# Turning xs with VectorE and ScalarE instead of TensorE in a Mamba-2 and attention trunk

## The chip, the cores and the metric

The kernel runs on one core of a Trainium2 chip. A core has five engines that work side by side, each through its own queue of instructions in order: TensorE (PE, matrix products, with its weight loads shown as PEld), VectorE (DVE), ScalarE (ACT), GpSimd (POOL) and SyncE (SP, which issues most of the DMAs). Operands lie in SBUF, a memory of 128 partitions; TensorE writes to PSUM, a second such memory. The metric is the device time of one execution in microseconds (us); lower is better.

## The reference

A trunk of two layers on x of 256 positions by 2048 features, float32. The first is a Mamba-2 mixer, the second a sliding-window attention mixer with shared keys and values; each ends in x <- LayerNorm(alpha * x + mixer(x)). The change lies in the first. Cut to what matters, that is:

```
zxbcdt = x @ w_in                     # 4096 z, 4096 xs, 1024 B, 1024 C, 64 dt
xbc = silu(causal_conv4(xs | B | C))
dt  = softplus(dt_raw + dt_bias);  da = dt * -exp(a_log)
cb      = C . B                       # per group: positions x positions
y_diag  = (cb * decay) @ (xs * dt)    # 8 heads a group, 64 features a head
y = y_diag + (the part from the chunk before) + xs * d_skip
y = y * silu(z);  y = rmsnorm_per_group(y) * norm_w;  out = y @ w_out
```

There are 8 groups of 8 heads, and two chunks of 128 positions. The kernel adds the part of the chunk before to the same product, with a decay over all 256 positions.

## The kernel before, in words

**Layout.** Activations of the first layer stand with features in the partitions and the 256 positions along the free axis. A weight block of 128 output features by 2048 inputs is loaded from DRAM in two halves of 128x1024 (tile wr), and each half is split into a high part that ScalarE rounds (wh, line L164) and a low part that VectorE subtracts (wl, L167). There are four buffers of wh, four of wl, six of wr. `load_next` keeps the splits two units ahead of their use.

**Blocks.** `block` makes one block of 128 features: 48 matmuls of 256 columns in `narrow` (L252), three for each of the 16 pieces of the input (high by high, low by high, high by low). Each group g has ten blocks: B, C, four blocks of xs (two heads each) and four of z. The first group takes three of its z blocks first, then B, C, the four xs and the last z. After a block of B, C or xs, `conv_silu` reads the PSUM tile: ScalarE scales (L492), VectorE adds three taps (L494), ScalarE takes tanh (L497) and VectorE closes (L498). After a block of z come L582 (ScalarE) and L583 (VectorE).

**What a group does.** `cb` multiplies C and B and masks (L590 to L592). `sum_decay` and `exp_decay` (L549, L557, ScalarE) make the decay e of the eight heads, `by_cb` (L597, VectorE) multiplies it by cb. `tr` (L607) turns the group's xs: TensorE transposes eight pieces of 128x128 into PSUM, and VectorE multiplies each of the four results by dt and writes it to xd (L612). `ymm` makes the products with xd as the stationary operand (L631), VectorE adds the skip part (L636, L642). `gate`, on GpSimd, multiplies by z and squares (L647 to L653); ScalarE and VectorE split the result into yH and yL (L661, L662). `norm` makes the scale of the group. The output blocks of the group (L323 to L325, 24 matmuls of 512 columns each) run in between the blocks of the next one.

**Order.** Two dictionaries, `plan` and `between`, say after (or within) which block each function is called. In the first group `tr` is called in block 11 (counted over all groups) and `ymm` after block 13; in the others `tr` after the group's eighth block and `ymm` after its tenth. The tile framework then orders the instructions of each engine by its own estimate of when their operands are ready, except for those that are held in program order (`pinned`, `keep_in_program_order`). The order of each engine's queue is fixed when the program is built.

**Buffers.** The tag yz has one buffer and holds the group's y; xd had four buffers of 256 columns. xs uses the tag sm, with seven.

Of the kernel before, what the change touches and what calls it, by code (L numbers as in the profile page):

```python
# [8 lines left out]
F32 = mybir.dt.float32  # L9
# [5 lines left out]
ALU = mybir.AluOpType  # L15
AX = mybir.AxisListType

P = 128
S = 256
# [36 lines left out]

BLOCKS = list(range(10))
BLOCKS0 = [6, 7, 8, 0, 1, 2, 3, 4, 5, 9]
CB_AT, TR_AT, Y_AT, NSM = 4, 7, 9, 7
B_ORDER = [("q", 0), ("g", 0), ("q", 1), ("g", 1), ("q", 2), ("o", 0), ("g", 2), ("q", 3),  # L60
           ("o", 1), ("g", 3), ("o", 2), ("o", 3)]

# [21 lines left out]
def trunk(ctx: ExitStack, tc: tile.TileContext, A: dict, out: bass.AP, dbg=None):  # L84
    nc = tc.nc
    PSUM = bass.MemoryType.PSUM

    def pool(name, bufs=1, side=None, space=None, stack=ctx):
        kw = {"space": space} if space is not None else {}
        return stack.enter_context(  # L90
            tc.tile_pool(name=name, bufs=bufs, side=side, reuse_waits="tile", **kw)
        )
# [9 lines left out]
    def nm(s):  # L102
        uid[0] += 1
        return f"{s}_{uid[0]}"

    def mm_tile():
        return mm_ps.tile([P, 512], F32, tag="mm", name=nm("mm"), bufs=4)

    def ax_tile():
        return ax_ps.tile([P, 512], F32, tag="ax", name=nm("ax"), bufs=4)  # L110

    cc = cst.tile([P, 1024], F32, tag="cc", name="cc")
    ident = cc[:, 0:128]
# [169 lines left out]
    ap = pool("ap", stack=w_stack)  # L283
# [25 lines left out]
    def pinned(m, pin):  # L309
        if pin:  # L310
            tc.keep_in_program_order(m)
# [86 lines left out]
    dtx = ap.tile([P, 2, NHD], F32, tag="dtx", name="dtx")  # L398
# [163 lines left out]
    gs = [G() for _ in range(NG)]  # L562
# [33 lines left out]
        e = es[g, hf]  # L596
        nc.vector.tensor_tensor(e[:], e[:], gs[g].cbm[:].unsqueeze(1).to_broadcast([P, 4, 384]), ALU.mult)  # L597

    def tr(g):
        st = gs[g]  # L600
        st.xd = {}
        for k in range(2):
            ps = ax_tile()
            for i in (2 * k, 2 * k + 1):
                for c in range(2):
                    o = (i % 2) * S + c * P
                    nc.tensor.transpose(ps[:, o : o + P], st.xs[i][:, c * P : (c + 1) * P], ident)  # L607
            for i in (2 * k, 2 * k + 1):
                o = (i % 2) * S
                xd = ap.tile([P, 2, 2, 64], F32, tag="xd", name=nm("xd"), bufs=4)  # L610
                hh = g * 8 + 2 * i
                m = nc.vector.tensor_tensor(  # L612
                    xd[:], ps[:, o : o + S].rearrange("p (c h d) -> p c h d", c=2, h=2),
                    dtx[:, :, hh : hh + 2].unsqueeze(3).to_broadcast([P, 2, 2, 64]), ALU.mult,
                )
                pinned(m, g == 0)
                st.xd[i] = xd

    def ymm(g):
        st = gs[g]  # L620
        st.yz = ap.tile([P, 4, S], F32, tag="yz", name=nm("yz"), bufs=1)
        for k in range(2):
            ps = ax_tile()
            for i in (2 * k, 2 * k + 1):
                o = (i % 2) * S
                xd = st.xd[i]
                for c in range(2):
                    cols = slice(o + c * P, o + S)
                    for r in range(2):
                        e = es[g, i // 2][:, 2 * (i % 2) + r, :]  # L630
                        nc.tensor.matmul(  # L631
                            ps[64 * r : 64 * r + 64, cols], xd[:, c, r, :], e[:, 256:] if c else e[:, :256],
                            start=c == 0, stop=c == 1,
                        )
            two = slice(2 * k, 2 * k + 2)
            nc.vector.tensor_tensor(  # L636
                st.yz[:, two, :], ps[:].rearrange("p (i q) -> p i q", i=2), els[g][:, two, :], ALU.mult
            )
            for i in (2 * k, 2 * k + 1):
                col = PC_D + g * 4 + i  # L640
                v = st.yz[:, i, :]
                nc.vector.scalar_tensor_tensor(v, st.xs[i][:], pc[:, col : col + 1], v, ALU.mult, ALU.add)  # L642
# [52 lines left out]
    def block(g, b):  # L695
# [15 lines left out]
        else:  # L711
            (in_b, in_c)[k](g, ps)

    visits = (turn_dt, cb, tr, ymm, norm)

    def group(g):
        for b in range(10):
# [75 lines left out]
    between = {}  # L793
# [6 lines left out]
    def at(t, fn, *a):  # L800
        plan.setdefault(t, []).append((fn, *a))
# [5 lines left out]
    for g in range(NG):  # L807
        t = 10 * g
        if g == 0:
            at(TD, turn_dt, *dts)  # L810
            at(4, load_decay, 0, 1)
            at(8, load_low, 0)
            pos = dict(cb=CB0, y=13)

            between[11] = [(tr, 0)]

            halves = [(5, 6, 7), (7, 8, 9)]
            by = (9, 10)
        elif g == 1:
            at(10, load_decay, 1, 0)  # L820
            at(10, load_decay, 1, 1)
            at(15, load_low, 1)
            pos = dict(cb=6, tr=TR_AT, y=Y_AT, norm=10 + CB_AT)

            halves = [(13, 14, 15), (15, 16, 16)]
            by = (16, 17)
        else:
            at(t - 5, load_decay, g, 0)
            at(t - 5, load_decay, g, 1)
            at(t, load_low, g)  # L830
            steps = t - 1
            pos = dict(cb=CB_AT, tr=TR_AT, y=Y_AT, norm=10 + CB_AT)
        for hf in range(2):
            if g < 2:
                sa, sb, ex = halves[hf]
                if (g, hf) != (1, 0):
                    at(sa, sum_decay, g, hf, 0, 2)
                at(sb, sum_decay, g, hf, 2, 4)
            else:
                at(steps + hf, sum_decay, g, hf)  # L840
                ex = steps + 1 + hf
            at(ex, exp_decay, g, hf)
        if g == 1:
            at(16, norm, 0)
        at(t + pos["cb"], cb, g)
        for hf in range(2):
            at(by[hf] if g < 2 else t + pos["cb"] + hf, by_cb, g, hf)
        if g > 0:
            at(t + pos["tr"], tr, g)
        at(t + pos["y"], ymm, g)  # L850
        if g == 0:
            at(t + pos["y"], sum_decay, 1, 0, 0, 2)
        for i in range(4):
            at(t + pos["y"], gate, g, i)
        if g > 0:
            at(t + pos["norm"], norm, g)
# [148 lines left out]
    for h in range(2):  # L1005
        ps = mm_tile()
# [277 lines left out]
    def cols(nb, c0=0, c1=512):  # L1284
        return slice(nb * 512 + c0, nb * 512 + c1)
# [67 lines left out]
    v = xr[:, 1, cols(3, 256)]  # L1353
# [102 lines left out]
```

## Time and profile before

| what | value |
|---|---|
| median of 3 runs | 987.62 us (987.59 to 988.2) |
| the profiled execution | 987.41 us, span 985.6 us |
| TensorE busy | 979.8 us (99%) |
| VectorE busy | 773.8 us (79%) |
| ScalarE busy | 611.9 us (62%) |
| GpSimd busy | 103.3 us (10%) |
| granted TensorE clock | 1.00 |
| transposes of L607 | 64, busy 8.3 us in all |
| scalings of L612 | 32, busy 11.9 us in all |

The profile is of one execution on the chip. A row of the groups of instructions names the line, the engine, the operation, what it writes and reads, the shape and the count; then its busy time in us and the mean duration of one in ns; then the engine's idle time just ahead of these instructions and what ended it. A row of the timeline has the start in us, the duration in us, and the instruction; "x10" means that ten in a row are merged. An instruction of an engine can begin before the last one has ended, so the distance between two starts can be shorter than a duration. The ends of matmuls are modelled; their starts are measured.

### The profile page before, as it was taken

How to read it: one execution, taken by the hardware profiler on the slowest of the kernel's cores; microseconds unless marked ns; L12 is line 12 of the kernel's file. 1: busy time of each engine (PE TensorE's matmuls, PEld its weight loads, DVE VectorE, ACT ScalarE, POOL GpSimd, SP SyncE). 2: the span in 40 equal slices, each digit the busy share in tenths (PEclk: the TensorE clock that was granted, in tenths of full speed). 3: DMA queues.
4: the chain of work that ended last, by engine and by line, in shares of the span. 5: the costliest groups of instructions: out<-in, count | busy, mean ns of one | idle time of the engine just before them, and what ended most of it. 6: DMA issues, size and time to landing. Idle time of an engine off the chain costs nothing.

```text
span 985.6 us, 18078 instructions
## 1 busy us (share of the span) xinstructions
PE 979.8 (99%) x7068; PEld 890.7 (90%) x7068; DVE 773.8 (79%) x1194; ACT 611.9 (62%) x1108; POOL 103.3 (10%) x137
## 2 busy tenths in 40 slices
PE   9999999999999999999999999999999999999998
PEld 8999989999999998999999999888898978978976
DVE  7898897877786787786787688789867678766786
ACT  7595866547655654663763665467467777764772
POOL 0001303004003001200300300303100000000003
PEclk9999999999999999999999999999999999999999
DMA  9788587565666656656657466458655646564642
GB/s 357 263 286 303 171 273 212 173 223 176 206 222 184 227 194 201 206 175 227 201 174 225 141 219 207 140 171 277 222 164 164 189 157 196 157 211 145 203 140 85
DMA packets 61556, 198.89 MB, mean 202 GB/s; under 512 B 6848, under 2 KB 11360, under 8 KB 61216
## 3 DMA queue, kind: packets, MB, share of 16 engines
q1 hardware_dynamic: 58528, 188.53, 58.4%
q0 software_dynamic: 2336, 8.69, 2.8%
q8 instruction: 55, 0.90, 0.4%
q10 hardware_dynamic: 608, 0.52, 0.2%
q14 instruction: 29, 0.24, 0.1%
HBM read 195.49 MB, written 2.23 MB: 201 GB/s over the span
## 4 chain that ended last, share of the span: by engine, by line
PE 99%; DVE 0%; DVEq 0%; issue 0%
PE mm L252 54%; PE mm L976 11%; PE mm L323 9%; PE mm L324 9%; PE mm L325 9%; PE ax L631 2%; PE ax L607 1%; PE ax L1116 1%; PE ax L1109 0%; PE ax L590 0%; PE mm L390 0%; PE ax L1233 0%; PE ax L1219 0%; PE ax L1066 0%; PE ax L907 0%; PE ax L372 0%
## 5 line engine op out<-in xcount | busy, mean ns | idle before, releaser
L167 DVE TENSOR_TENSOR wl<-wr,wh 128x1024 fp32r<-128x1024 f32 (+2 forms) x338 | 393.8, 1184 | 104.2 <-ACT wh L164 100.9
L164 ACT ACTIVATE wh<-wr 128x1024 fp32r<-128x1024 f32 (+2 forms) x338 | 333.1, 1011 | 146.6 <-PE mm L252 58.4
L252 PE MATMUL mm<-xH,wh 128*128 128x256 f32 x1280 | 355.4, 278 | 0.0
L252 PE MATMUL mm<-xL,wh 128*128 128x256 f32 x1280 | 354.1, 277 | 0.0
L252 PE MATMUL mm<-xH,wl 128*128 128x256 f32 x1280 | 353.9, 276 | 0.0
L252 PEld LDWEIGHTS mm<-xH,wh 128*128 128x128 f32 x1280 | 240.7, 188 | 1.8 <-issue 0.5
L252 PEld LDWEIGHTS mm<-xL,wh 128*128 128x128 f32 x1280 | 240.6, 188 | 1.0
L252 PEld LDWEIGHTS mm<-xH,wl 128*128 128x128 f32 x1280 | 240.5, 188 | 0.0
L323 PE MATMUL mm<-wh,yH 128*128 128x512 f32 x256 | 101.4, 396 | 0.0
L324 PE MATMUL mm<-wh,yL 128*128 128x512 f32 x256 | 99.8, 390 | 0.0
L325 PE MATMUL mm<-wl,yH 128*128 128x512 f32 x256 | 99.7, 389 | 0.0
L647 POOL TENSOR_TENSOR yz<-yz,z 128x256 f32<-128x256 f32 x32 | 32.7, 1032 | 470.7 <-DVE yz L642 470.7
L252 PE MATMUL mm<-x1H,wh 128*128 128x256 f32 x256 | 71.9, 281 | 0.0
L494 DVE SCALAR_TENSOR_TENSOR cv<-mm,pc,cv 128x255 f32<-128x255 f32 x144 | 68.8, 478 | 3.3 <-ACT cv L492 1.9
L252 PE MATMUL mm<-x1L,wh 128*128 128x256 f32 x256 | 71.1, 278 | 0.0
L252 PE MATMUL mm<-x1H,wl 128*128 128x256 f32 x256 | 71.0, 278 | 0.0
L976 PE MATMUL mm<-wh,x1H 128*128 128x512 f32 x160 | 63.1, 394 | 0.0
L976 PE MATMUL mm<-wl,x1H 128*128 128x512 f32 x160 | 61.8, 389 | 0.0
L976 PE MATMUL mm<-wh,x1L 128*128 128x512 f32 x160 | 60.9, 390 | 0.0
L323 PEld LDWEIGHTS mm<-wh,yH 128*128 128x128 f32 x256 | 48.1, 188 | 10.3 <-DVE z L583 1.0
L325 PEld LDWEIGHTS mm<-wl,yH 128*128 128x128 f32 x256 | 48.1, 188 | 10.2
L332 DVE SCALAR_TENSOR_TENSOR xr<-mm,r,xr 128x512 f32<-128x512 f32 x64 | 47.1, 746 | 11.7 <-PE mm L325 7.3
(228 smaller groups left out, 1375.8 us busy)
## 6 DMA issues: line engine op xcount, KB each, us to landing
wr<-in_wa SPq DMA_DIRECT2D x154, 512.0 KB, 5.0
wr<-in_wo SPq DMA_DIRECT2D x64, 512.0 KB, 4.4
wr<-in_wq SPq DMA_DIRECT2D x32, 512.0 KB, 4.4
wr<-in_wg SPq DMA_DIRECT2D x31, 512.0 KB, 5.0
wr<-in_wb SPq DMA_DIRECT2D x16, 512.0 KB, 4.5
wr<-in_wb SPq DMA_DIRECT2D x32, 256.0 KB, 3.8
rb<-rscr SPq DMA_DIRECT2D x11, 512.0 KB, 4.1
wr<-in_wkv SPq DMA_DIRECT2D x8, 512.0 KB, 5.1
```

The lines of the kernel that those rows point to most:

```text
L164: m = nc.scalar.activation(h[:, sl], v, AF.Copy)
L167: m = nc.vector.tensor_tensor(l[:, sl], v, h[:, sl].bitcast(F32), ALU.subtract)
L252: m = nc.tensor.matmul(ps, a, b, start=first and i == 0, stop=last and i == 2)
L323: pinned(nc.tensor.matmul(ps, aH[:, k, hs], u.h[:, ks], start=k == 0 and add is None, stop=False), pin)
L324: pinned(nc.tensor.matmul(ps, aL[:, k, hs], u.h[:, ks], start=False, stop=False), pin)
L325: pinned(nc.tensor.matmul(ps, aH[:, k, hs], u.l[:, ks], start=False, stop=k == 3), pin)
L332: nc.vector.scalar_tensor_tensor(v, ps, rms[:, h : h + 1], v, ALU.mult, ALU.add)
L494: nc.vector.scalar_tensor_tensor(a[:, sft:], ps[:, : S - sft], w(3 - sft), a[:, sft:], ALU.mult, ALU.add)
L607: nc.tensor.transpose(ps[:, o : o + P], st.xs[i][:, c * P : (c + 1) * P], ident)
L631: nc.tensor.matmul(ps[64 * r : 64 * r + 64, cols], xd[:, c, r, :], e[:, 256:] if c else e[:, :256], start=c == 0, stop=c == 1,)
L647: nc.gpsimd.tensor_tensor(v, v, st.z[i][:], ALU.mult)
L976: m = nc.tensor.matmul(ps[:], (x1H, x1L, x1H)[i][:, kk, hs], (u.h, u.h, u.l)[i][:, ks], start=(kk, i) == (0, 0), stop=ui == 3 and (k, i) = ...
```

## The change

xs is no longer turned by TensorE. `turn_xs` has VectorE transpose each of the four xs tiles of a group (128x256) in blocks of 32x32 into zx, a tile in yz's buffer. A block transpose leaves each block in the partitions where it was, so `carry_xs` copies the blocks to the partitions where they belong: 16 copies of 32 partitions by 256 elements on ScalarE, from quarter i of the partitions of zx to quarter j of those of xd. `scale_xs` then multiplies the whole of xd (128x1024) by dt in place, with one instruction of VectorE. xd is one tile with one buffer, and `ymm` reads it from there. The turn stands after block 9 in the first group and after the seventh block of each other group; the copies stand there and after the one or two blocks behind it; the scaling is two blocks behind the turn (three in the first group, where it is held in program order).

```
-    def tr(g):
-        ...
-                    nc.tensor.transpose(ps[:, o : o + P], st.xs[i][:, c * P : (c + 1) * P], ident)
-        ...
-                m = nc.vector.tensor_tensor(
-                    xd[:], ps[:, o : o + S].rearrange("p (c h d) -> p c h d", c=2, h=2),
-                    dtx[:, :, hh : hh + 2].unsqueeze(3).to_broadcast([P, 2, 2, 64]), ALU.mult,
-                )
+    def turn_xs(g):
+        st = gs[g]
+        st.zx = ap.tile([P, 4, 8, 32], F32, tag="yz", name=nm("zx"), bufs=1)
+        for i in range(4):
+            nc.vector.transpose(st.zx[:, i].rearrange("p f b -> p (f b)"), st.xs[i][:])
+        st.xd = ap.tile([P, 2, 4, P], F32, tag="xd", name=nm("xd"), bufs=1)
+    def carry_xs(g, js):
+        st = gs[g]
+        z = st.zx[:].rearrange("p i (c j) b -> p j c i b", c=2)
+        for j in js:
+            for i in range(4):
+                nc.scalar.copy(st.xd[32 * j : 32 * j + 32, :, :, 32 * i : 32 * i + 32], z[32 * i : 32 * i + 32, j])
+    def scale_xs(g):
+        v = gs[g].xd[:].rearrange("p c i (h d) -> p c (i h) d", h=2)
+        d = dtx[:, :, g * 8 : g * 8 + 8].unsqueeze(3).to_broadcast([P, 2, 8, 64])
+        pinned(nc.vector.tensor_tensor(v, v, d, ALU.mult), g == 0)
...
-                            ps[64 * r : 64 * r + 64, cols], xd[:, c, r, :], e[:, 256:] if c else e[:, :256],
+                            ps[64 * r : 64 * r + 64, cols], st.xd[:, c, i, 64 * r : 64 * r + 64], e[:, 256:] if c else e[:, :256],
...
-            between[11] = [(tr, 0)]
+            xs_at = 9
...
         if g > 0:
-            at(t + pos["tr"], tr, g)
+            xs_at = t + 6
+        at(xs_at, turn_xs, g)
+        for n, js in enumerate(((0,), (1,), (2, 3)) if g < 2 else ((0, 1), (2, 3))):
+            at(xs_at + n, carry_xs, g, js)
+        at(xs_at + 2 + (g == 0), scale_xs, g)
```

In the changed kernel the block transposes are line L604, the copies L613 and the scaling L618; the later lines of the file move by three.

More of the change, by code (lines that the diff above doesn't have):

```diff
@@ L58 @@
 BLOCKS0 = [6, 7, 8, 0, 1, 2, 3, 4, 5, 9]
-CB_AT, TR_AT, Y_AT, NSM = 4, 7, 9, 7
+CB_AT, Y_AT, NSM = 4, 9, 7
 B_ORDER = [("q", 0), ("g", 0), ("q", 1), ("g", 1), ("q", 2), ("o", 0), ("g", 2), ("q", 3),
@@ L597, in by_cb @@
         nc.vector.tensor_tensor(e[:], e[:], gs[g].cbm[:].unsqueeze(1).to_broadcast([P, 4, 384]), ALU.mult)
-    def tr(g):
+    def turn_xs(g):
         st = gs[g]
[L601 to L612, printed above, removed]
-                    xd[:], ps[:, o : o + S].rearrange("p (c h d) -> p c h d", c=2, h=2),
-                    dtx[:, :, hh : hh + 2].unsqueeze(3).to_broadcast([P, 2, 2, 64]), ALU.mult,
-                )
-                pinned(m, g == 0)
-                st.xd[i] = xd
+        st.zx = ap.tile([P, 4, 8, 32], F32, tag="yz", name=nm("zx"), bufs=1)
[12 more added lines that the diff above has]
+        pinned(nc.vector.tensor_tensor(v, v, d, ALU.mult), g == 0)
     def ymm(g):
@@ L625, in ymm @@
                 o = (i % 2) * S
-                xd = st.xd[i]
                 for c in range(2):
@@ L712, in block @@
             (in_b, in_c)[k](g, ps)
-    visits = (turn_dt, cb, tr, ymm, norm)
+    visits = (turn_dt, cb, ymm, norm)
     def group(g):
@@ L822, in trunk @@
             at(15, load_low, 1)
-            pos = dict(cb=6, tr=TR_AT, y=Y_AT, norm=10 + CB_AT)
+            pos = dict(cb=6, y=Y_AT, norm=10 + CB_AT)
             halves = [(13, 14, 15), (15, 16, 16)]
@@ L831, in trunk @@
             steps = t - 1
-            pos = dict(cb=CB_AT, tr=TR_AT, y=Y_AT, norm=10 + CB_AT)
+            pos = dict(cb=CB_AT, y=Y_AT, norm=10 + CB_AT)
         for hf in range(2):
```

## The prediction

> **What bounds the kernel now.** I read the page's busy shares first, then its chain of work.
>
> ```profile
> span 985.6 us, 18078 instructions
> PE 979.8 (99%) x7068; PEld 890.7 (90%) x7068; DVE 773.8 (79%) x1194; ACT 611.9 (62%) x1108; POOL 103.3 (10%) x137
> ...
> PE 99%; DVE 0%; DVEq 0%; issue 0%
> ```
>
> TensorE is the bound, and the chain that ended last runs on it from end to end. So a matmul taken away is worth its full pitch, and a microsecond in which TensorE waits costs a microsecond. The other engines count only where they make it wait. The busy time of each engine by stretch shows where that is near (columns: PE, PEld, DVE, ACT, POOL busy and instructions, clock, DMA share, GB/s):
>
> ```profile
> 58.00:76.00 18.00, 18.00 (x159) 17.95 (x158) 16.85 (x22) 16.12 (x28) 1.06 (x2) 1.00 0.84 284
> 76.00:94.00 18.00, 18.00 (x167) 17.13 (x166) 15.24 (x27) 8.31 (x12) 0.00 (x0) 1.00 0.93 354
> 310.00:390.00 80.00, 80.00 (x620) 75.50 (x619) 60.56 (x80) 45.89 (x68) 8.49 (x10) 1.00 0.62 199
> ```
>
> In the first group (about 58 to 94 us) VectorE is 85 to 94% busy, and ScalarE 90% in the first half. A later group (310 to 390) leaves VectorE 19 us and ScalarE 34 us idle. The change will be decided in the first group.
>
> **What the change removes: eight transposes a group on TensorE.** The timeline of TensorE around those of one group:
>
> ```profile
> 287.14 0.28 PE L252 MATMUL mm<-xH,wl 128*128 128x256 f32 x1
> 287.25 1.04 PE L607 MATMUL ax<-cc,xs 128*128 128x128 f32 x8
> 288.05 0.36 PE L252 MATMUL mm<-xH,wh 128*128 128x256 f32 x1
> 288.25 0.28 PE L252 MATMUL mm<-xL,wh 128*128 128x256 f32 x1
> 288.37 0.28 PE L252 MATMUL mm<-xH,wl 128*128 128x256 f32 x1
> ```
>
> Eight transposes hold the array from 287.25 to 288.05, 0.80 us. The matmul after them takes 0.20 us to the next start where 0.113 is usual (288.25 to 288.37, and 48 of them make a block of 5.45 us): 0.08 more. So 0.88 us a group, 8 x 0.88 = 7.0 us. Nothing else on TensorE changes in number: the products of L631 keep their shapes.
>
> **What it adds on VectorE and ScalarE.** The groups of instructions by shape (busy us, mean ns | idle before):
>
> ```profile
> L612 DVE TENSOR_TENSOR xd<-ax,dtx 128x256 f32<-128x256 f32 x32 | 11.9, 419 | 6.9 <-PE ax L607 6.8
> L1158 DVE STREAM_TRANSPOSE z<-p 128x1024 f32<-128x1024 f32 x8 | 9.9, 1239 | 0.0
> L1150 DVE TENSOR_TENSOR p<-p,sm 128x1024 f32<-128x1024 f32 x8 | 9.8, 1226 | 0.3
> L1177 ACT COPY ptw<-z 32x256 f32<-32x256 f32 x56 | 22.6, 404 | 9.6 <-DVE z L1158 8.9
> L1129 ACT COPY p<-ax 128x256 f32<-128x256 f32 x16 | 4.7, 382 | 0.0
> L661 ACT ACTIVATE yH<-yz,pc 128x256 fp32r<-128x256 f32 x32 | 16.3, 510 | 33.2 <-POOL yz L647 33.2
> L647 POOL TENSOR_TENSOR yz<-yz,z 128x256 f32<-128x256 f32 x32 | 32.7, 1032 | 470.7 <-DVE yz L642 470.7
> ```
>
> VectorE loses four L612 a group (0.33 us apart, 1.32) and gains four block turns and one scaling. A turn of 1024 columns takes 1.24 us, as the elementwise L1150 does; so one of 256 is put at L612's 0.42, 0.33 apart. The scaling of 128x1024 from SBUF is L1150's 1.23. Sum: 1.3 + 1.15 - 1.3 = 1.2 us more a group. ScalarE gains 16 copies of 32x256. L1177 is the same kind, 32 partitions to 32 others, at 0.404. L1129, which writes in pieces of 32 columns as the new copies do, takes 0.382 over 128 partitions; so the pieces cost nothing. The dearest row for 256 columns from SBUF is L661's 0.51, my upper bound. How close together do they run?
>
> ```profile
> 735.60 2.00 ACT L164 ACTIVATE wh<-wr 128x1024 fp32r<-128x1024 f32 x2
> ...
> 739.89 4.12 ACT L1177 COPY pt<-z 32x256 f32<-32x256 f32 x10
> 744.03 2.10 ACT L164 ACTIVATE wh<-wr 128x128 fp32r<-128x128 f32 x3
> ```
>
> Two L164 (1.05 each by their group) end in 2.00: the second starts 0.1 before the first ends. Ten copies take 4.14 to the next start, 0.414 each: none starts before the last one ended. The Trainium skill, "VectorE: DVE Perf Modes", section "Two Vector instructions with no wait between them", says that an instruction whose operands start in another quarter of the partitions than the last one's is held until that has finished. It tells this of VectorE alone, and the row shows it on ScalarE; read as the page has it, the copies would run 0.31 apart and my sum would be 984.2 instead of 986.2. I take the row: 16 x 0.414 = 6.6 us a group, as every new copy changes its quarter.
>
> No DMA is added, removed or moved; SP's and GpSimd's queues are as before. The new buffer zx shares yz's slot, so VectorE's first turn of a group waits for GpSimd's gating of the group before. That is eleven instructions of at most L647's 1.03, so some 11 us after the products; the first turn follows the next group's third block, 16 us after them: hidden.
>
> **Groups 2 to 7.** The copies stand behind ScalarE's reading of the seventh block, the scaling behind them. In one group that reading and the products were these:
>
> ```profile
> 282.10 0.36 ACT L582 ACTIVATE z<-mm 128x256 f32<-128x256 f32 x1
> ```
>
> ```profile
> 304.60 2.82 PE L631 MATMUL ax<-e,xd 128*64 128x256 f32 x32
> ```
>
> Between them lie 22 us. The copies' 6.6, two weight splits of 0.95 among them and 1.2 of scaling need 10. ScalarE has 34 us idle a group to take 6.6 from, so the splits keep ahead too, and the gain of 0.88 is kept in each group.
>
> **Group 0, where it is lost.** The timelines of TensorE, ScalarE and VectorE before:
>
> ```profile
> 88.00 2.82 PE L631 MATMUL ax<-e,xd 128*64 128x256 f32 x32
> ```
>
> ```profile
> 68.11 0.42 ACT L497 ACTIVATE xs<-cv 128x256 f32<-128x256 f32 x1 [1.69 <-DVE cv L494]
> ...
> 72.42 1.99 ACT L164 ACTIVATE wh<-wr 128x1024 fp32r<-128x1024 f32 x2
> 74.31 0.55 ACT L492 ACTIVATE cv<-mm,pc 128x256 f32<-128x256 f32 x1
> 74.76 1.05 ACT L164 ACTIVATE wh<-wr 128x1024 fp32r<-128x1024 f32 x1
> 79.11 0.42 ACT L497 ACTIVATE bt<-cv 128x256 f32<-128x256 f32 x1 [3.29 <-DVE cv L494]
> ```
>
> ```profile
> 79.56 0.43 DVE L498 SCALAR_TENSOR_TENSOR bt<-bt,cv 128x256 f32<-128x256 f32 x1 [0.55 <-ACT bt L497]
> 79.91 1.41 DVE L612 TENSOR_TENSOR xd<-ax,dtx 128x256 f32<-128x256 f32 x4
> ...
> 90.46 0.42 DVE L498 SCALAR_TENSOR_TENSOR xs<-xs,cv 128x256 f32<-128x256 f32 x1 [0.54 <-ACT xs L497]
> ```
>
> TensorE reaches the first group's products at 88.00. In the changed order ten matmuls of the next block stand ahead of them, so it gets there at 88.00 - 0.88 + 10 x 0.113 = 88.2. What it needs is the scaled xd. Before, L612 had made that by 81.3, out of PSUM. In the changed order of VectorE the scaling stands behind L498 of the second group's first xs block, which ran at 90.46. If nothing ahead of it moved, the scaling would end at 90.46 + 0.34 + 1.23 = 92.0: 3.8 us too late. And it does move:
> - ScalarE: eight copies, one split's two halves and three copies now stand ahead of L492 (74.31), five more copies behind it. Eleven copies add 4.6; a split half (0.95) has gone behind L492; the idle 1.69 at 68.11 is gone, since VectorE now does the stencil of the fourth xs block earlier. L492 starts at 74.31 + 4.6 - 0.95 - 1.6 = 76.4.
> - Its three stencils on VectorE wait for each other (0.55 each), then the tanh waits behind five copies (2.1) and a split half: L498 of bt at about 81.2, 1.6 later than 79.56.
> - From there to L498 of xs were 10.9 us, nearly all busy. Four L612 leave (1.3) and a fifth split half comes in (1.1): again some 10.9, so 92.2.
> The scaling runs from 92.5 to 93.7 and TensorE starts the products at 93.8: **a gap of 5.6 us**.
>
> **Group 1** has the least to spare after that. A low half at 122.02 is done at 124.37, its first reader starts at 125.80:
>
> ```profile
> 122.02 2.35 DVE L167 TENSOR_TENSOR wl<-wr,wh 128x1024 fp32r<-128x1024 f32 x2
> ```
>
> ```profile
> 125.80 0.28 PE L252 MATMUL mm<-xH,wl 128*128 128x256 f32 x1
> ```
>
> 1.4 us spare. Four turns come in ahead and 13 copies in a row; TensorE comes 4.8 us later (the gap less 0.88). Walked in the same way, 0.4 us is left: no wait, but barely.
>
> **The sum**, on the profiled execution: 987.41 (span 985.6 and 1.8 around it) - 7.0 + 5.6 = 986.0. That execution stands 0.2 below the median of the runs, 987.62; so **986.2 us**, 0.14% faster. A measurement of this kernel can tell about 0.2%, so this is no change.
>
> **Bounds.** Each 0.1 us on a copy moves the gap by 1.6. Copies 0.31 apart give a gap of 3.6 and 984.2; copies of 0.51 one of 7.2 and 987.8. Turns as dear as 0.78 would cost 2 us, partly in group 1.
>
> **The rivals.**
> - The clock falls in the gap (0.30). TensorE starts the program at half pace:
>
> ```profile
> 1.00 2.95 PE L372 MATMUL ax<-zero 128*128 128x512 bf16 x7 [1.00 <-DVE zero L360]
> ...
> 5.35 0.41 PE L252 MATMUL mm<-xH,wh 128*128 128x256 f32 x1
> 5.56 0.37 PE L252 MATMUL mm<-xL,wh 128*128 128x256 f32 x1
> 5.77 0.28 PE L252 MATMUL mm<-xH,wl 128*128 128x256 f32 x1
> 5.89 0.28 PE L252 MATMUL mm<-xH,wh 128*128 128x256 f32 x1
> ```
>
> Starts are 0.21 apart until 5.77, then 0.12, after work from 1.0 on: 4.8 us at half pace, 2.4 us lost. TensorE idles 5.8 us in the whole span before (979.8 of 985.6), most of it at its ends, so no row tells how long an idle stretch has to be. The matmul stream goes on at full pace after the waits of tenths of a microsecond that the rows show, and starts at half pace after the long rest before the program; 5.6 us lies between, so the chance is not far below the forecast's. If it is enough, 986.2 + 2.4 = 988.6 (987.4 to 990). The Trainium skill, "TensorE: Matmul & The Clock Gate", section "Why this matters for your kernels", warns of idle gaps over some 3 us: one idle window puts the clock back to half. By that rule the forecast would be 988.6 in those runs in which a whole window falls into the gap; the start of the trace agrees, and no run here shows the fall.
> - A second gap in group 1 (0.18), the case on the slower side: VectorE over 0.4 us later than walked at the split of 122 us, because 13 copies in a row keep ScalarE's halves back. Each us beyond 0.4 costs one; from 1.8 us the kernel is slower than before, from 3.8 by over 0.2%. It speaks for it that the spare time was 1.4 even before; against it, that ScalarE and VectorE work on while TensorE stands in the first gap. 988 to 993.
> - The gap is smaller or absent (0.14): copies overlap (984.2), or the scaling comes in time (980.6). Against it is the order: L618 stands behind an instruction at 90.46.
>
> **How the numbers follow.** The forecast, with gap and full clock, has 0.38 and its own range 985.2 to 987.6. 980.6 and 993 are the outer ends; cut to eight in ten: 983 to 991. Faster than 985.6: most of the small-gap case and a quarter of the forecast, 0.25. Slower than 989.6: two thirds of the second gap and the upper part of the clock case with some room for what I don't see, 0.25. Within: 0.50.
>
> **What would show it.** No L607 on TensorE; L631 of group 0 starting near 93.8, with some 5.6 us idle ahead, released by VectorE's L618; L613 x16 in each group with starts 0.41 apart; each later group 0.88 us shorter. TensorE's starts behind the gap 0.21 apart would be the clock; an idle stretch near 129 the second gap; L618 before 90 or L613 far from 0.40 would make the walk wrong.

## The result, and the profile after

The changed kernel takes 989.82 us, median of 20 runs (987.17 to 991.69); the kernel before, on the same chip, 987.80 (987.35 to 989.18). The ratio is 1.0018, with a 95% interval of 1.0011 to 1.0025: slower by 2 us, where 986.2 had been forecast. The profiled execution took 990.41 us, 3.0 more than that of before.

The head of the page and its chain that ended last, changed kernel:

```profile
span 988.6 us, 18074 instructions
...
PE 975.7 (99%) x7004; PEld 885.2 (90%) x7004; DVE 781.8 (79%) x1202; ACT 662.7 (67%) x1236; POOL 103.8 (10%) x137
...
PE 93%; ACT 3%; DMA 2%; DVE 1%; issue 1%; DVEq 0%; ACTq 0%
```

TensorE has its 64 transposes less and is 4.1 us less busy, yet the span is 3.0 longer. The chain, which ran on TensorE from end to end before, now goes through ScalarE, a DMA and VectorE first: somewhere TensorE waited for them. The timeline of TensorE has the place:

```profile
88.61 0.28 PE L252 MATMUL mm<-xH,wh 128*128 128x256 f32 x1
96.02 5.39 PE L631 MATMUL ax<-e,xd 128*64 128x256 f32 x32 [7.12 <-DVE xd L618]
101.33 0.38 PE L252 MATMUL mm<-xL,wh 128*128 128x256 f32 x1
```

Two things stand in it. From the last matmul to group 0's products are 7.40 us, released by the scaling L618: a gap, where the forecast had one, but longer than its 5.6. And the 32 products take 5.39 us, where they took 2.82 before. The table of stretches says why (columns: length, PE busy and instructions, granted clock, DMA share, GB/s):

```profile
80.00:91.00 11.00, 8.89 (x79) 1.00 0.81 269
91.11:101.35 10.24, 5.33 (x33) 0.50 0.78 276
101.35:120.00 18.65, 18.65 (x154) 1.00 0.43 133
```

The clock fell to one half 2.5 us behind the start of the last matmul ahead of the gap and came back 5.3 us after work had begun again. The sum closes on the spans: 7.0 saved, 7.40 - 0.11 lost in the gap, 5.39 - 2.82 = 2.57 lost at half pace; -7.0 + 7.3 + 2.6 = +2.9, and the spans differ by 3.0. The mean granted clock was 0.994 to 0.997 in every one of the 20 runs, and 0.999 to 1.0 in 93 of the 95 runs of before that were taken beside the experiments (0.998 and 0.997 in the other two). The products keep the line L631 in the changed file.

### The profile page after: what moved, and what is told of

Same layout as the page of the kernel before. It is cut to its first block, busy times and chain, and to the rows that moved or that the text cites. A ratio compares the mean times of both kernels' runs of the same rounds, so it can differ in the third digit from the quotient of the medians.

```text
span 988.6 us, 18074 instructions
## 1 busy us (share of the span) xinstructions
PE 975.7 (99%) x7004; PEld 885.2 (90%) x7004; DVE 781.8 (79%) x1202; ACT 662.7 (67%) x1236; POOL 103.8 (10%) x137
## 4 chain that ended last, share of the span: by engine, by line
PE 93%; ACT 3%; DMA 2%; DVE 1%; issue 1%; DVEq 0%; ACTq 0%
PE mm L252 49%; PE mm L979 11%; PE mm L323 9%; PE mm L324 9%; PE mm L325 9%; PE ax L631 2%; ACT wh L164 1%; DMA rb<-rscr 1%; ACT xd L613 1%; PE ax L1119 1%; ACT e L549 1%; DMA wr<-in_wa 0%; PE ax L1112 0%; DVE wl L167 0%; PE mm L390 0%
## 5 line engine op out<-in xcount | busy, mean ns | idle before, releaser
L497 ACT ACTIVATE xs<-cv 128x256 f32<-128x256 f32 x32 | 13.3, 416 | 69.7 <-DVE cv L494 69.7
L325 PEld LDWEIGHTS mm<-wl,yH 128*128 128x128 f32 x256 | 48.1, 188 | 10.2
```

Source lines behind the costliest of these rows:

```text
L325: pinned(nc.tensor.matmul(ps, aH[:, k, hs], u.l[:, ks], start=False, stop=k == 3), pin)
L497: nc.scalar.activation(dst, a[:], AF.Tanh)
```

## The experiments

Two claims of the forecast were to be tried first, the 0.88 us a group and the loss in group 0; then what each part of the loss costs. The theory held after the result: the gap comes from the place of the scaling on VectorE, and the clock falls in it and costs as well. The main rival: the gap alone costs, and the half clock is covered by something else.

### Groups 1 to 7 alone, group 0 alone

```
+            if g == 0:
+                between[11] = [(tr, 0)]     # TensorE's turn, as before, into the single xd
+            else:
                 at(xs_at, turn_xs, g)
                 ...
```

The second kernel has it the other way round: group 0 the new way, the others by `tr`.

> The first group keeps its transposes on TensorE (written into the one xd tile); groups 1 to 7 are as in the changed kernel. Theory (the loss is the first group's late scaling and the clock that falls in the wait): seven gains of 0.88 us, no wait of several us, clock 1.00; 987.7 - 6.2 = 981.5, at most 982.5. Rival (the 16 copies a group cost ScalarE, and so TensorE, something in every group): the loss is spread over the groups, seven eighths of it stay, 989 to 990.

> Only the first group is turned in the new way; groups 1 to 7 keep their transposes. Theory: one gain of 0.88, a wait of 5.6 to 7.4 us ahead of the first group's products and 2 to 4 us for the fallen clock; 994 to 998. Rival (cost in every group): one eighth of the change's effect, 987.5 to 988.5.

Measured, beside 987.75 us for the kernel before on the same chip: groups 1 to 7 alone 982.74 us (982.68 to 984.62, 5 runs), ratio 0.9952 (0.9940 to 0.9965), at a clock of 0.999 to 1.0. Group 0 alone 995.92 (995.55 to 997.06, 4 runs), ratio 1.0083 (1.0069 to 1.0097). So the change gains 5 us in seven groups and loses 8 in the first. Group 0 alone shows the gap and the half pace again, in TensorE's timeline (L649 and L636 are the products and the scaling in this file):

```profile
95.74 5.22 PE L649 MATMUL ax<-e,xd 128*64 128x256 f32 x32 [6.98 <-DVE xd L636]
```

By the same sum: -0.9 for its eight transposes, 7.25 - 0.11 for the gap, 5.22 - 2.82 for the pace, together +8.6; the medians differ by 8.2.

Groups 1 to 7 gain 7 x 0.88 = 6.2 less a wait of 1.16 us that comes up in group 1 (122.32 to 123.48):

```profile
122.32 0.39 PE L325 MATMUL mm<-wl,yH 128*128 128x512 f32 x1
123.48 0.50 PE L323 MATMUL mm<-wh,yH 128*128 128x512 f32 x1 [0.77 <-DVE xr L332]
```

The usual distance between two such matmuls is 0.23 us, so the wait costs 0.9: 987.75 - 6.2 + 0.9 = 982.5, and 982.74 was measured. In the changed kernel the first gap hides this wait. So its +2.0 us is group 0's +8.2 less the whole 6.2 of the seven others.

### The scaling of group 0 set free, or planned one block earlier

```
-        pinned(nc.vector.tensor_tensor(v, v, d, ALU.mult), g == 0)
+        pinned(nc.vector.tensor_tensor(v, v, d, ALU.mult), False)
```

```
-        at(xs_at + 2 + (g == 0), scale_xs, g)
+        at(xs_at + 2, scale_xs, g)
```

> All eight groups new; the first group's scaling is not held in program order, so that it stands on VectorE ahead of L498 of block B of the second group. Theory: the wait ahead of the first group's products goes (xd ready by about 81 us, before TensorE comes at 87), the clock stays at 1.00; 980.6 if TensorE waits nowhere else, 984 if the later gating of the first group keeps its norm (a wait of up to 2.7 us near 109 us). Rival (cost in every group): the place of one scaling changes little, 988 to 990.

> All eight groups new; the first group's scaling is called one block earlier (after block 11) and still held in program order, so that it stands behind L498 of block C of the second group, five microseconds ahead of its place in the changed kernel. Theory: the wait shrinks from 5.6 to 7.4 us to some 1.6 to 3.4, too short for the clock to fall in most runs: 982 to 986. If even a wait of 2 to 3 us lets the clock fall, 2 to 3 us more and a granted clock below 1.00. Rival (cost in every group): 988 to 990.

Measured: free 986.36 us (985.18 to 989.15, 11 runs), ratio 0.9988 (0.9979 to 0.9997); one block earlier 986.36 (984.53 to 988.17, 10 runs), ratio 0.9983 (0.9974 to 0.9992). Moving this one instruction of VectorE takes the first gap away, or leaves 2.04 us of it (87.18 to 89.21). But more than 5 of the 7 us do not arrive, where 980.6, or 984 with one wait, had been expected for the first and 982 to 986 for the second. With the scaling free TensorE waits twice, behind 106.6 and 124.7:

```profile
109.95 0.61 PE L671 MATMUL ax<-cc,sq 128*128 128x1 f32 x4 [3.07 <-POOL sq L653]
...
127.66 0.50 PE L323 MATMUL mm<-wh,yH 128*128 128x512 f32 x1 [2.56 <-DVE xr L332]
```

In this execution the sum is -7.0 + 3.24 + 2.72 = -1.0 (each wait less the usual distance, 0.11 and 0.23), and 986.76 was measured, 1.0 below 987.75. One block earlier, the first is gone and the second stays, 2.94 us behind 122.95, with a half clock behind it. The table of stretches of that kernel:

```profile
110.00:122.00 12.00, 12.00 (x78) 1.00 0.60 183
125.59:129.00 3.41, 3.11 (x7) 0.50 0.20 25
129.00:140.00 11.00, 11.00 (x74) 1.00 0.75 241
```

So the first gap had hidden waits behind it. The rest of the work of groups 0 and 1 is later too, and TensorE did not notice while it was late itself: VectorE's L636 of group 0, behind which gating and norm follow, ran at 92.94 us before, at 95.67 with the scaling one block earlier and at 97.47 with it free. Part of this belongs to the execution and not to the kernel, since ScalarE's second xs block, an early mark of how late an execution runs, stood at 57.81, 58.25 and 60.28. So these two profiles do not show that the wait at 106.6 depends on the place of the scaling.

### What the half clock costs: products of filling in the gap

```
+    mask_fill = cc[:, 0:512]
     def ymm(g):
         ...
             ps = ax_tile()
+            for _ in range(N if (g, k) == (0, 0) else 0):
+                nc.tensor.matmul(ps[:], ident, mask_fill, start=True, stop=True)
```

N is 1, 14 and 7. They write the PSUM tile that group 0's products then overwrite, and keep TensorE at work while it waits. Each turned out to be two matmuls, so 14 ran far past the gap; 7 were tried after that.

> The changed kernel with one product of filling (128x512, fp32, the identity by a constant, into the PSUM tile that group 0's products then overwrite) on TensorE just ahead of group 0's products; nothing is left out. It is the control of the next run: the filling's own place and hazards, but no cover. A filling product of this size takes 0.43 us at full clock (429 ns from start to start of such products in the trace of after). It lies in time in which TensorE waits for xd anyway. Theory (the idle time costs twice, by itself and by the half clock behind it): as the changed kernel, 989 to 991, clock 0.994 to 0.997. Rival (the clock costs nothing beside the gap): the same 989 to 991. Both expect a half clock of one to three stretches of 3.41 us behind the gap.

> The same with 14 products of filling, 14 x 0.43 = 6.0 us of TensorE's work, so that of the 7.4 us from one matmul to the next some 1.4 us stay idle; nothing is left out. xd comes no sooner, so the products of group 0 start at the same time as with one. Theory (the idle time lets the clock fall, and the work behind it at half pace costs about 2.6 us): the clock stays 1.00 through 88 to 105 us, and the time is 2 to 3 us below that of the run with one product, 986.5 to 988.5. Rival (only the gap costs): the same time as with one product within 0.5 us, 989 to 991.

> Seven products of filling ahead of group 0's products; nothing is left out. The run with 14 showed that each is two matmuls of 0.43 us (28 x 0.435 = 12.18 us), so it covered the gap and 4 to 5 us more; seven are 6.1 us, which end at about 93.7 us, where xd of group 0 was ready at 93.7 to 96.0 us in the traces so far. The gap's end stays where it was, and what is left idle is 0 to 2.3 us. Theory (the half clock behind the gap costs about 2.6 us): clock 1.00 in all runs, and the time is 2 to 3 us below that of the changed kernel on the same chip, 986.5 to 988.0. Rival (the idle time costs only itself): within 0.7 us of the changed kernel, 989 to 991, at a clock of 1.00.

> The changed kernel itself, beside the last one on the same chip; nothing is left out. Both theories: 989 to 991. Its profile is a second look at the gap: if the gap's length follows the end of the first convolutions (ready time of xd 35.9 to 36.0 us behind ScalarE's second xs block, as in three traces so far), a second xs block at 57.7 to 60.3 us gives a gap of 5.1 to 7.6 us, and the clock is below 0.998 in every run.

> One product of filling, again, as the control on the same chip for the next run; nothing is left out. It differs from the changed kernel also in that some eight matmuls of the block that TensorE is in when it reaches group 0's products stand behind these and not ahead (0.9 us at 0.113 each), so that it, and not the changed kernel, is what the run with seven is to be held against (ten such matmuls there, 0.2 us more). Both theories: 988.5 to 990.5, clock 0.994 to 0.997.

> Seven products of filling, again, beside the control; nothing is left out. Theory (the half clock costs): group 0's products took 5.35 us at half clock and 2.82 at full clock in the runs so far, 2.5 us; 0.65 us of it comes back as a wait of group 1 (129.91 us in the run with seven), and 0.2 stands against it for the two matmuls; so 1.4 to 2.0 us below the control, 987.0 to 988.7. Rival (only the idle time costs): within 0.5 us of the control.

| kernel | us, median (range, runs) | ratio (95%) | clock |
|---|---|---|---|
| one | 989.30 (987.99 to 993.45, 10) | 1.0024 (1.0014 to 1.0034) | 0.994 to 0.997 |
| one, again | 989.78 (987.11 to 991.71, 10) | 1.0018 (1.0006 to 1.0029) | 0.995 to 0.997 |
| seven | 988.54 (986.99 to 990.30, 11) | 1.0010 (1.0002 to 1.0019) | 0.997 to 1.0 |
| seven, again | 988.33 (986.92 to 990.77, 12) | 1.0005 (0.9996 to 1.0014) | 0.998 to 1.0 |
| fourteen | 992.57 (992.39 to 992.62, 4) | 1.0048 (1.0035 to 1.0062) | 0.999 to 1.0 |
| the changed kernel again | 989.26 (987.52 to 991.49, 11) | 1.0015 (1.0005 to 1.0025) | 0.995 to 0.997 |

TensorE's timeline with one product of filling, and below it with seven:

```profile
87.57 1.02 PE L628 MATMUL ax<-cc 128*128 128x512 f32 x2
...
93.71 5.35 PE L635 MATMUL ax<-e,xd 128*64 128x256 f32 x32 [4.89 <-DVE xd L618]
98.99 0.39 PE L252 MATMUL mm<-xH,wl 128*128 128x256 f32 x1
```

```profile
87.97 6.17 PE L628 MATMUL ax<-cc 128*128 128x512 f32 x14
96.18 2.82 PE L635 MATMUL ax<-e,xd 128*64 128x256 f32 x32 [2.04 <-DVE xd L618]
98.93 0.38 PE L252 MATMUL mm<-xH,wh 128*128 128x256 f32 x1
```

With filling that lasts, 2.04 us of idle time are left and the products take 2.82 us; with one product they take 5.35. The second profiles agree: 2.49 us and 2.82, against 5.20 us and 5.08. The clock fell because TensorE idled, and keeping it at work on nothing of use holds it up: the mean clock was 0.999 to 1.0 in 21 of the 23 runs with seven, and at most 0.997 in all 20 with one. In time, the runs with seven are shorter than those with one by 1.2 us, as the means of 20 and 23 runs go (989.83 with one and 988.61 with seven; twice the standard error of the difference is 0.8). The runs with one are all of one chip, those with seven of two; on the chip that had both side by side the medians differ by 1.4 us, as the last expectation had it (1.4 to 2.0), and the means by 1.3, with twice the standard error at 1.2. The first series with seven alone would not have told: its median lies 0.7 us below that of the changed kernel beside it, between the theory's 2 to 3 and the rival's at most 0.7. The theory's 2 to 3 us were too much: of the 2.5 us of pace, 0.4 come back as a wait in group 1 (0.65 behind 129.91 us, where 0.23 is usual), and 0.2 go to the two matmuls by which the order differs. So the rival that the clock costs nothing falls, though by a small margin. The run with 14 has no gap and no half clock; its 28 matmuls of 0.435 us are the whole of it: 987.8 - 7.0 + 12.2 = 993.0, measured 992.57.

The second profile of the changed kernel has a gap of 7.13 us (89.10 to 96.23), products of 4.50 us and the half clock from 92.84 for 6.83 us.

### Why 7.4 and not 5.6

The run with one product of filling shows the forecast's walk almost to the digit, and the changed kernel's own profile shows it 2.3 us later. ScalarE and VectorE with one product of filling:

```profile
75.10 1.24 ACT L613 COPY xd<-zx 32x256 f32<-32x256 f32 x3
76.36 0.56 ACT L492 ACTIVATE cv<-mm,pc 128x256 f32<-128x256 f32 x1
76.95 2.06 ACT L613 COPY xd<-zx 32x256 f32<-32x256 f32 x5
```

```profile
81.27 0.42 DVE L498 SCALAR_TENSOR_TENSOR bt<-bt,cv 128x256 f32<-128x256 f32 x1
...
92.10 0.42 DVE L498 SCALAR_TENSOR_TENSOR xs<-xs,cv 128x256 f32<-128x256 f32 x1 [0.54 <-ACT xs L497]
92.44 1.22 DVE L618 TENSOR_TENSOR xd<-xd,dtx 128x1024 f32<-128x1024 f32 x1
```

The forecast had L492 at 76.4, bt at 81.2, xs at 92.2 and the scaling at 92.5. The changed kernel, ScalarE and VectorE:

```profile
72.06 3.30 ACT L613 COPY xd<-zx 32x256 f32<-32x256 f32 x8
75.38 2.01 ACT L164 ACTIVATE wh<-wr 128x1024 fp32r<-128x1024 f32 x2
77.42 1.24 ACT L613 COPY xd<-zx 32x256 f32<-32x256 f32 x3
78.68 0.56 ACT L492 ACTIVATE cv<-mm,pc 128x256 f32<-128x256 f32 x1
79.26 2.06 ACT L613 COPY xd<-zx 32x256 f32<-32x256 f32 x5
```

```profile
94.40 0.42 DVE L498 SCALAR_TENSOR_TENSOR xs<-xs,cv 128x256 f32<-128x256 f32 x1 [0.54 <-ACT xs L497]
94.74 1.22 DVE L618 TENSOR_TENSOR xd<-xd,dtx 128x1024 f32<-128x1024 f32 x1
```

Eight copies in 3.32 us are 0.415 each, as forecast, so the copies are not what is late. In the eight profiles that have the scaling at this place it begins 34.67 to 34.71 us behind ScalarE's tanh (L497) of the second xs block, and that tanh ran between 57.66 and 60.27 (57.81 before). Ahead of it ScalarE waits for a DMA, the broadcast of the decay's rows. Before, and then the changed kernel:

```profile
48.86 1.20 ACT L549 ACTIVATE e<-rb,rtk 128x256 f32<-128x256 f32 x3 [3.25 <-DMA rb<-rscr]
```

```profile
50.80 1.20 ACT L549 ACTIVATE e<-rb,rtk 128x256 f32<-128x256 f32 x3 [4.93 <-DMA rb<-rscr]
```

In those eight profiles the first of these began at 48.55 to 51.09, and the two earliest of them (48.55, 49.01) go with the two earliest scalings (92.34, 92.44). The broadcast is not the whole of it: from there to the tanh it was 8.7 to 9.9 us. Before the change such a delay was covered (xd was ready at 81.3 us and wanted at 88.0); now it is passed on to the gap. What makes the broadcast land early or late was not tried.

### Group 1: whose wait is it?

```
+            elif g == 1:
+                at(t + 7, tr, g)            # groups 0 and 1 as before, 2 to 7 the new way
```

```
-                nc.scalar.copy(st.xd[...], z[...])
+                (nc.gpsimd.tensor_copy if g < 2 else nc.scalar.copy)(st.xd[...], z[...])
```

The second kernel has the scaling free as well.

> Groups 0 and 1 turned by TensorE as before, groups 2 to 7 the new way; nothing is left out. Theory A (a group from 2 on gives its whole 0.88 us; group 1's new path ends later than TensorE wants it and gives back about the 1.16 us of the wait that groups 1 to 7 showed): no wait at 122 us, TensorE's work less by 6 x 0.88 = 5.3 us, 987.75 - 5.3 = 982.5 (982.0 to 983.2), the same as groups 1 to 7 (982.74) within 0.5 us. Theory B (group 1's change is free, and its wait came from elsewhere): the wait of about 1 us stays, and the time is 0.9 above that of groups 1 to 7, 983.6.

> The changed kernel with the scaling of xs free in the order (as in e3), and with the 32 copies of groups 0 and 1 on GpSimd in place of ScalarE; the other groups as changed; nothing is left out. Theory (the waits of 3.35 us at 106.6 for the norm of group 0 and of 2.95 us at 124.7 for the split of yz of group 1 come from ScalarE's 2 x 6.6 us of copies, which push its later work of the two groups back): with those off ScalarE the wait at 124.7 falls below 1 us, and the time is about 983.5 to 985 if GpSimd brings xd in time. Rival (they come from VectorE's own longer work and order): both waits stay within 0.7 us of what they were, and the time is 986 to 987. If GpSimd's copies take much longer than ScalarE's 0.41 us, xd of group 0 is late and a new gap of several us stands ahead of group 0's products; then the run says nothing on ScalarE.

Groups 2 to 7 alone take 982.29 us (981.76 to 983.04, 5 runs), ratio 0.9946 (0.9934 to 0.9959), as theory A has it: no wait, and 6 x 0.88 = 5.3 us gained in full. Its chain is TensorE's again:

```profile
PE 99%; DVE 0%; DMA 0%; ACT 0%; DVEq 0%; issue 0%
```

With GpSimd's copies 987.31 us (985.87 to 991.42, 10 runs), ratio 0.9999 (0.9987 to 1.0011). The wait of group 1 is 1.11 us, smaller, but not for the reason given: VectorE's order there is the same as with groups 1 to 7,

```profile
122.61 0.43 DVE L604 STREAM_TRANSPOSE zx<-xs 128x256 f32<-128x256 f32 x1
122.97 1.72 DVE L597 TENSOR_TENSOR e<-e,cbm 128x1536 f32<-128x1536 f32 x1
124.61 1.09 DVE L604 STREAM_TRANSPOSE zx<-xs 128x256 f32<-128x256 f32 x3
125.62 1.37 DVE L332 SCALAR_TENSOR_TENSOR xr<-mm,r,xr 128x512 f32<-128x512 f32 x2
```

and TensorE came later by a wait of 2.94 us at 106 and 3.41 us of half clock behind it. GpSimd's 16 copies in group 0 took 14.1 us, 0.88 each on average, and VectorE stood for 3.83 us waiting for them. So this run says nothing on ScalarE, and what makes the wait at 106 is left open. What it does show is the order: the four turns (L604), with L597 between them, stand ahead of L332, which empties the PSUM tile that TensorE's next output block needs. With groups 2 to 7 alone no turn stands there, the first L332 is ahead of L597, and it comes 3 us earlier than with groups 1 to 7. VectorE of groups 1 to 7, then of groups 2 to 7:

```profile
122.71 1.37 DVE L332 SCALAR_TENSOR_TENSOR xr<-mm,r,xr 128x512 f32<-128x512 f32 x2
```

```profile
119.67 0.74 DVE L332 SCALAR_TENSOR_TENSOR xr<-mm,r,xr 128x512 f32<-128x512 f32 x1
```

That was tried by itself: groups 1 to 7 the new way, group 1's turn planned one block later, which brings the turns ahead of the norm's arithmetic.

```
             else:
+                xs_at += g == 1
                 at(xs_at, turn_xs, g)
```

> Groups 1 to 7 the new way, as in the first experiment, but group 1's turn, copies and scaling are planned one block later; VectorE's order then has the four turns ahead of the norm's arithmetic (beside the third and fourth xs blocks) and no longer between that and L332, which empties the PSUM of the output blocks. Nothing is left out. Theory (TensorE's wait of 1.16 us at 122 us came from the turns standing ahead of L332 on VectorE: 122.71 us there, 119.67 with group 1 unchanged): the wait is gone, and group 1 gives its 0.88 us: 981.4 to 982.0, 0.5 to 0.9 below groups 2 to 7, with L332 at about 120 us. Rival (it came from ScalarE's copies of group 1): the copies are as many and stand as close behind the turns, so a wait of about 1 us stays, and the time is 982.5 to 983.

> Groups 2 to 7 the new way, again, as the control on the same chip; nothing is left out. Both: 982.0 to 982.8, no wait of TensorE between 100 and 130 us.

Measured: 982.74 us (980.97 to 984.09, 6 runs), ratio 0.9942 (0.9922 to 0.9962); the control 982.11 (981.92 to 982.62, 6 runs), ratio 0.9939 (0.9923 to 0.9955). The wait at 122 us is gone, so it came from the order with the turns ahead of L332 (which runs at 121.20 now). But the time is not lower, since 9 us on there is another, of 1.52 us. TensorE and ScalarE of this kernel (L631 is the copy there):

```profile
130.68 0.28 PE L252 MATMUL mm<-xH,wl 128*128 128x256 f32 x1
132.20 0.50 PE L323 MATMUL mm<-wh,yH 128*128 128x512 f32 x1 [1.24 <-DVE z L583]
```

```profile
125.78 4.56 ACT L631 COPY xd<-zx 32x256 f32<-32x256 f32 x11
130.36 1.06 ACT L164 ACTIVATE wh<-wr 128x1024 fp32r<-128x1024 f32 x1
131.32 0.36 ACT L582 ACTIVATE z<-mm 128x256 f32<-128x256 f32 x1
```

Eleven copies keep ScalarE from reading the next z block, VectorE follows, and the PSUM tile comes free late. So both theories hold one wait each: the turns the first, the copies the second. The second is read from this one trace and was not tried by itself. These runs show nothing to win in group 1: with groups 2 to 7 the medians are 982.1 and 982.3, and both versions that add group 1 have 982.7. That difference is not clear of the noise (0.6 us between the means of 11 runs each, twice the standard error 0.7). Groups 2 to 7 alone has the lowest medians of all kernels run, 0.6% faster than before.

## Why the prediction was wrong

- **0.88 us a group: right.** Groups 2 to 7 give 5.4 to 5.5 us, where 6 x 0.88 = 5.3 were forecast (987.82 against 982.29, and 987.52 against 982.11).
- **Prices: right.** Copies 0.415 us apart (0.414 forecast), turns 0.44 (0.42), the scaling 1.22 (1.23); ScalarE is 50.8 us busier in all, 8 x 16 copies of 0.40. The Trainium skill, "VectorE: DVE Perf Modes", section "Two Vector instructions with no wait between them", tells of held instructions on VectorE alone; the trace shows ScalarE's copies held in the same way, eight of 0.40 us in 3.32. Each of them reads from another quarter than the last one; that this is the cause was not tried. The same page, section "Rules for kernel authors", says to turn a 128x128 tile on TensorE where the result may go to PSUM. Here it depends on the group: in group 0 the runs agree, by 8.2 us; in group 1 no difference is clear of the noise; in groups 2 to 7 the other way is 0.88 us a group faster, since TensorE is the bound there and the other engines' added work is hidden.
- **Group 0, the place and the cause of the gap: right.** L618 stands behind L498 of group 1's first xs block; set free, the gap is gone.
- **Its size: off by 1.8 us, in the step "a gap of 5.6 us".** The walk was right for an execution that starts as early as the one it was made on (with one product of filling 57.73 against 57.81, and the scaling at 92.44 against 92.5). But it took its starting time from one profile, and this start varies by 2.6 us between executions, 57.7 to 60.3. The profile of before had an early one (57.81), that of the changed kernel a late one (60.07), and by so much its scaling is later: 94.74 where 92.5 was forecast. TensorE came 0.4 us later than forecast as well, which leaves the 1.8. A delay that cost nothing before, since TensorE had work, is passed on in full once TensorE waits at that place.
- **The clock: the step that failed.** The forecast took "gap and full clock" for likelier (0.38) than "the clock falls in the gap" (0.30). It fell in every run of the changed kernel, and the sum had put nothing for it. By the figures on windows in the last section there was no choice between the two: a gap of the forecast's own size, over 5 us idle, always leaves 2.5 us or more idle in one window, where 2.04 were enough. Its price of 2.4 us was right for the products (1.7 to 2.6 us), and in the whole time 1.2 us of it is left when the clock is held up. The Trainium skill, "TensorE: Matmul & The Clock Gate", section "Why this matters for your kernels", had been weighed only as a chance; the trace agrees in that the clock falls, 7.40 us of gap and 10.24 us of half clock, but it fell after 2.2 us of idle time and not after some 3. With the two sizes the sum is 986.0 + 1.8 + 2.6 = 990.4, and the profiled execution took 990.41.
- **Group 1: half right.** In the changed kernel it has no wait, as forecast. But "0.4 us is left" held only because the first gap had put TensorE back: without that gap 1.2 to 2.9 us of wait come up, by the turns on VectorE, and behind them by the copies on ScalarE. The second rival had VectorE late at the split of 122 us because copies in a row keep ScalarE's halves back. The waits that came are others: the first is the output blocks' PSUM behind the turns, the second a block of z that ScalarE reads late behind the copies.

## What to carry to other kernels

When a change opens a wait on the bounding engine, price the wait from several executions of the kernel before, not from one: a lateness that was covered is passed on in full. Add the half clock to each gap on TensorE that leaves it idle for some 4.1 us or more, and count it as a chance from 2.0 us on. And where the same edit stands in many groups, judge it group by group: here the six pipelined groups gain all of it, the first loses more than they gain, the second wins nothing that the runs can show, and leaving these two as they were is the better kernel.

## What the runs showed of the hardware

The half clock comes in steps of 3.41 us: 10.24, 6.83 and 3.41 us were seen. In five profiles with a gap of 5.2 to 7.4 us it lasted two or three steps. Gaps near 3 us went both ways: behind 2.94 us of gap the clock fell twice (one block earlier, GpSimd's copies), behind 2.64, 2.95, 3.09 and 3.35 it did not. A gap shorter than one step can thus be enough.

The traces show what decides. In each of the 16 profiles all changes of the clock lie whole steps of 3.413 us apart, from the first to the last. They divide the span into windows, and the clock falls at the end of a window in which TensorE idled enough. The last window ahead of the fall, in the changed kernel and with the scaling one block earlier:

```profile
87.70:91.11 3.41, 1.19 (x11) 1.00 0.83 256
122.17:125.59 3.42, 1.17 (x6) 1.00 0.72 272
```

Two windows behind which it did not fall, with the scaling free (the one with the most idle time of all such windows; two of them share the gap of 3.35 us) and with group 0 alone (whose clock fell one window later):

```profile
105.39:108.81 3.42, 1.49 (x14) 1.00 0.35 84
87.01:90.42 3.41, 1.75 (x16) 1.00 0.84 247
```

Over all profiles, every window at full clock with 2.04 us idle or more ended in a fall (seven within the program, 16 at its end, where TensorE runs out of work), and none with 1.93 or less did (idle time by the modelled ends of the matmuls). By these figures an idle stretch of some 4.1 us always puts enough into one of two windows. What a shorter one costs depends on where it falls on them: in nine of the eleven runs with the scaling free the mean clock was 0.996 to 0.998, so there it fell in other executions. No window has to be idle as a whole. That was not expected: "TensorE: Matmul & The Clock Gate" of the Trainium skill, section "Part 1: The HAM clock gate (the "warmup" mystery)", speaks of at least one idle window of about 3.4 us. The step's length agrees with that; the 2.94 us gaps do not, nor does the fall behind a window with 2.2 us of idle time.

GpSimd's copies of 32x256 took two prices. The table of stretches of that kernel over the 16 copies of group 0 (columns: PE, PEld, DVE, ACT, POOL busy and instructions, clock, DMA share, GB/s):

```profile
68.47:78.67 10.20, 10.20 (x92) 10.20 (x91) 10.20 (x10) 5.97 (x8) 9.92 (x7) 1.00 0.98 328
78.67:82.60 3.93, 3.93 (x37) 3.93 (x36) 0.11 (x1) 0.00 (x0) 3.56 (x9) 1.00 1.01 362
```

Seven copies took 10.2 us, 1.46 each, while VectorE worked without a pause; nine took 3.93, 0.44 each, while VectorE stood and waited. ScalarE's were 0.415 apart beside a busy VectorE.
